# Low parts of the weights by an adding transfer, and a denser order of side work, in a one-core decoder trunk

## The chip, the cores and the metric

The kernel runs on one core of one Trainium2 chip. The metric is the device time of one execution in microseconds (us). The engines of a core are TensorE (PE, with its weight loads shown as PEld), VectorE (DVE), ScalarE (ACT), GpSimd (POOL) and SyncE (SP), which here issues most transfers (DMAs). Sixteen DMA engines serve all queues.

## The reference

One step of a hybrid decoder layer, for a prompt (16 meta tokens and 512 new ones) and 8 sample tokens that share the weights, 536 columns in all. Everything is float32.

```python
xn = rmsnorm(x, norm_gain)
h = einsum('btd,de->bte', xn, w_in)                 # 2048 -> 8704
q, k, v, z_a, u, z_s, g_a, g_s = split(h)
q, k = rope(rmsnorm(q)), rope(rmsnorm(k))
o_attn = sink_attention(q, k, v, window 128 + meta, sinks)   # 16 heads on 4 kv heads
y_ssm, state = s5_branch(u, ...)                    # diagonal complex scan, 64 groups x 64 states
y_ssm = gelu(y) * sigmoid(gelu(y) @ w_glu + b_glu)
br_a = (o_attn * silu(z_a)) @ w_attn_out
br_s = (y_ssm * silu(z_s)) @ w_ssm_out
y = x + (sigmoid(g_a) * br_a + sigmoid(g_s) * br_s) @ w_out
```

The outputs are y, the new keys and values, the final states, and the samples' updated windows.

## The kernel before

**Weights.** All weight matrices lie in one array `w` of units, each 128 x 8 x 128 values (512 KB). 176 units are streamed by `Stream`, and 32 more (w_out) by `Quads`, which forms 7 products for 8. TensorE multiplies float32r operands, so each weight is split into a high part `whi` (the cast) and a low part `wlo` (weight minus high part), and so are the activations (`xh`, `xl`). A product is three matmul passes: hi·hi, hi·lo and lo·hi. One unit is 48 matmuls of 260 or 268 columns on the line of `mm` (L901). `Stream.piece` makes a unit: SyncE loads `raw` (L783), ScalarE casts (L784), VectorE subtracts (L785). `Stream.get` makes units two ahead of the one that is handed out.

**Stages.** In the first 45 us the x tiles arrive, are scaled by the norm's gain and split, and three blocks are multiplied as they come (L988). Then follow blocks of two units each, in the order of the table `ORDER1`: `x` (a gate block, written to DRAM as gD), `u` (input of eight state-space blocks, each starting a generator `ssm`) and `h` (q, k and v rows, written to DRAM as rawD). Before, 42 blocks stand in that table. The remaining x blocks run beside attention. Then come w_glu (reads Y1), w_ssm_out (Y2), w_attn_out (A) and, through `Quads`, w_out (the line of `pr`, L1264).

**Side work.** `Background` holds generators in lanes. After each unit `mm` calls `bg.step(budget)`, which lets the generators issue work up to a number of units of VectorE time (BUDGET, and BUDGET2 to BUDGET4 in later stages). A generator yields the cost of what it has just issued, or None to end its turn. `ssm` is one such generator, `attention` another; `Attn.sample`, the sample tokens' attention, runs in the second lane. It reads the cached keys and values in pieces of 288 KB, and its loads are issued by GpSimd.

**Order.** The engines' queues are in order. The scheduler of the framework sets the order of each queue from the program order, a priority (the weights' work carries a high one) and its own estimate of time. SyncE's loads and stores, of weights and of side work, stand in one queue and reuse eight completion semaphores in turn, so a DMA waits until the eighth before it has landed.

**A state-space block.** u is evacuated to `uf`, split, written to DRAM (uD) and read back as `U` in another layout; `U` is read by the matmuls of L345 and L346; the scan runs on VectorE; L388, L392 and L396 form the block's output. GpSimd clears borders of U and H by memsets (L333, L340).

**Attention's start.** When the last state-space block is written, its memory is released and attention's tiles are loaded by SyncE: constants (k_cos and others), then for each of two pairs of kv heads the tiles sb, sw and rb of the keys, and the first query tiles. Two V tiles (L497) follow, which VectorE copies to `vb` (L501) and TensorE transposes (L505, L506). The first score matmul is L537.

Of the kernel before, what the change touches and what calls it, by code (L numbers as in the profile page):

```python
# [14 lines left out]
P = 128  # L15
# [208 lines left out]
def ssm_consts(nc, pool, psum, R, D, ub, a_bT, a_bN, a_cT, bdm):  # L224
# [26 lines left out]

    bN = pool.tile([P, 4, 2, 32], F32, name="bN")
    nc.sync.dma_start(out=bN, in_=a_bN[:, ps])
# [25 lines left out]
    v.tensor_tensor(out=k0, in0=bc(kp[:, 0, 0:32], 1, 4), in1=bc(bdm, 2, 32), op=ALU.mult)  # L279
    kh = pool.tile([P, P], F32R, name="kh")  # L280
    kl = pool.tile([P, P], F32R, name="kl")
    k0f = k0.rearrange("p a h -> p (a h)")
# [138 lines left out]
class Attn:  # L421
# [203 lines left out]
    def sample(self, a_sink, a_kc, a_vc):  # L625
# [3 lines left out]
        for c in range(2):  # L629
            cols = slice(4 * c, 4 * c + 4)  # L630
            src = self.raw[:, :, c, 264:268].rearrange("n p j -> p n j")
            nc.gpsimd.dma_start(out=x[:, :, cols], in_=src)
            for q in range(4):
                b = 32 * (q ^ 1)
                nc.gpsimd.dma_start(out=sw[32 * q:32 * q + 32, :, cols], in_=src[b:b + 32])
            for e in range(2):
                half = slice(64 * e, 64 * e + 64)
                for dst, r, w in ((rb[half, 4:12, cols], self.rq, 260), (rb[half, 0:2, cols], self.rk, CH)):
                    s = r[e::2, c * w + w - 4:c * w + w]
                    nc.gpsimd.dma_start(out=dst, in_=s.unsqueeze(0).to_broadcast([64] + list(s.shape)))  # L640
        co, si = C["cos"][:, 0, 264:265], C["sin"][:, 0, 264:265]
# [17 lines left out]
        for b in range(8):  # L659
            nc.gpsimd.dma_start(out=qD[:, b], in_=qt[8 * b:8 * b + 8])  # L660
        for i in range(2):
            for b in range(2):
                nc.gpsimd.dma_start(out=kD[i, :, b], in_=kt[16 * i + 8 * b:16 * i + 8 * b + 8])
        self.kD = kD
        q = pool.tile([P, 64], F32, name="qv", bufs=1)
        nc.gpsimd.dma_start(out=q, in_=qD.rearrange("s b (e d) -> (s b e) d", e=2))
        self.qv = q
        self.sk = pool.tile([P, 1], F32, name="sk", bufs=1)
        nc.gpsimd.dma_start(out=self.sk, in_=a_sink)
        yield 0.0  # L670
# [3 lines left out]
        def load(i, c, src):  # L674
            t = pool.tile([P, CK, 64], F32, name="cache")
            n = CK if c < 15 else CK - 1
            self.after = nc.gpsimd.dma_start(out=t[:, 0:n], in_=src[:, c * CK:c * CK + n]).ins
            if n < CK:
                new = self.kD[i].rearrange("s b (e d) -> (s b e) d", e=2)
                for r in range(4):  # L680
                    nc.gpsimd.dma_start(out=t[r::4, n], in_=new)
            return t
# [83 lines left out]
class Stream:  # L766


    def __init__(self, tc, nc, pool, w, ahead=2):
        self.tc, self.nc, self.pool, self.w, self.ahead = tc, nc, pool, w, ahead  # L770
        self.made, self.i, self.parts = 0, 0, {}

    def tiles(self, i, pool=None):
        raw = self.pool.tile([P, 8, P], F32, name="raw", bufs=3)
        hi = (pool or self.pool).tile([P, 8, P], F32R, name="whi", bufs=3)
        lo = (pool or self.pool).tile([P, 8, P], F32R, name="wlo", bufs=3)
        self.parts[i] = (hi, lo)
        return raw, hi, lo

    def piece(self, i, t, ks):  # L780
        nc = self.nc
        raw, hi, lo = (a[:, ks] for a in t)
        nc.sync.dma_start(out=raw, in_=self.w[i][:, ks])  # L783
        nc.scalar.copy(out=hi, in_=raw)  # L784
        self.dve = nc.vector.tensor_tensor(out=lo, in0=raw, in1=hi.bitcast(F32), op=ALU.subtract).ins  # L785
# [13 lines left out]
class Quads:  # L799
# [8 lines left out]

    def __init__(self, tc, nc, w, first, n, pool):
        self.tc, self.nc, self.w, self.first, self.n, self.pool = tc, nc, w, first, n, pool  # L810
        self.more = None
        self.loaded, self.made, self.i = 0, 0, 0
        self.raw, self.parts = {}, {}

    def load(self, upto):
        while self.loaded < min(upto, 4 * self.n):
            k = self.loaded
            pool, bufs = (self.pool, 3) if k % 7 < 3 else (self.more, 4)
# [36 lines left out]
def trunk(tc, A, O):  # L855
# [27 lines left out]
    nc.scalar.activation(out=warm, in_=warm, func=AF.Tanh)  # L883

    xn = tc.tile_pool(name="xn", bufs=1)
    xp = xn.__enter__()
# [3 lines left out]
    def mm(n, hi_of, lo_of, w0, budget=None, pool=mmp, name="mm"):  # L890
# [3 lines left out]
        for h in range(n):  # L894
# [47 lines left out]
    tmp = spp.__enter__()  # L942
    with tc.tile_pool(name="xld", bufs=2, side="right") as xld:
        ones = xld.tile([P, P], F32, name="ones", bufs=1)
        v.memset(ones, 1.0)
# [5 lines left out]
        def square(kt):  # L951
            sq = acc if kt == 0 else xld.tile([P, 2, CH], F32, name="xsq")
# [65 lines left out]
        for i, t in early:  # L1018
            evac(i, t)
        nx = NB0 + 2  # L1020
    C = {"idn": idn}
    bdm, dsk, bglu = const("bdm"), const("dsk"), const("bglu")
# [116 lines left out]
    def attended():  # L1139

        nonlocal late
        for i, (cache, out) in enumerate((("wk", "s_win_k"), ("wv", "s_win_v"))):
            with tc.issue_after(at.after):
                nc.gpsimd.dma_start(out=O[out][:, 0:127], in_=A[cache])
            nc.gpsimd.dma_start(out=O[out][:, 127], in_=at.kD[i].rearrange("s b d -> s (b d)"))
        att.__exit__(None, None, None)
# [74 lines left out]
    if late is None:  # L1221
        list(attended())
    xn.__exit__(None, None, None)
    Ah, Al = parts["a"]


    cbp = ent(tc.tile_pool(name="cbp", bufs=1))
    cb = []
    qs = Quads(tc, nc, A["w"], NUNIT, 8, wp)
    for i in range(16):  # L1230
# [208 lines left out]
```

## Time and profile before

| | |
|---|---|
| median of 3 runs | 1316.57 us (1316.45 to 1318.03) |
| profiled execution | 1317.95 us, of which the span of the profile is 1316.1 us |
| granted TensorE clock | 0.997 of full speed |
| busy | PE 1300.7 us, DVE 1003.5, ACT 443.5, POOL 52.4 |
| DMA | 209.70 MB, of which GpSimd's queue 13.89 MB |

A profile shows one execution. "Busy" is the time in which an engine executes; matmuls are pipelined, so a busy TensorE need not run at its best rate, and the number of matmuls that start in a window says more. In a timeline a row gives the start, the time to the end of the last of its instructions, the engine, the source line, the operation, output and inputs, a count, and in brackets the idle time ahead of it with what ended it. "SPq" is SyncE issuing a transfer, which lands later.

### The profile page before, as it was taken

The page shows a single profiled execution, that of the slowest core. Times are in us where ns is not written, and L with a number is a line of the kernel's source. Part 1 is how long each engine was busy: PE and PEld are TensorE (multiplying, and loading weights), DVE is VectorE, ACT ScalarE, POOL GpSimd, SP SyncE. Part 2 cuts the span into 40 slices and gives each one's busy share as a digit, 9 for nine tenths or more (in the row PEclk, how much of TensorE's full clock was granted, in tenths as well). Part 3 has the DMA queues.
Part 4 walks back from the last instruction along what each step waited for, and adds up shares of the span by engine and source line. Part 5 has one row for each costly group of instructions (what it writes and reads, how often), then busy time and mean ns, then how long its engine had stood idle before and what let it go on. Part 6 is the DMA issues. An engine that isn't in the chain of part 4 may idle for free.

```text
span 1316.1 us, 26574 instructions
## 1 busy us (share of the span) xinstructions
PE 1300.7 (99%) x10804; PEld 1259.9 (96%) x10804; DVE 1003.5 (76%) x1882; ACT 443.5 (34%) x742; POOL 52.4 (4%) x124
## 2 busy tenths in 40 slices
PE   9999999999999999999989999999999999999998
PEld 8999999999999999999989999999999999999998
DVE  7887788887969697968577688686885357888775
ACT  8322221223222222222254433334433133344342
POOL 0000000000000000000400210100011000000000
PEclk9999999999999999999989999999999999999999
DMA  8347363626353444343874346446677666554441
GB/s 268 123 136 212 104 186 115 187 92 184 110 166 116 155 122 153 97 152 125 190 228 131 107 153 193 131 133 205 194 226 247 203 194 189 159 199 142 151 145 50
DMA packets 95962, 209.70 MB, mean 159 GB/s; under 512 B 16556, under 2 KB 34972, under 8 KB 95808
## 3 DMA queue, kind: packets, MB, share of 16 engines
q1 hardware_dynamic: 91168, 194.11, 46.8%
q0 software_dynamic: 4672, 13.89, 4.0%
q8 instruction: 85, 1.39, 0.4%
q14 instruction: 37, 0.30, 0.1%
HBM read 175.32 MB, written 34.74 MB: 160 GB/s over the span
## 4 chain that ended last, share of the span: by engine, by line
PE 91%; DMA 3%; DVE 2%; ACT 1%; SPq 1%; issue 0%; POOL 0%; DVEq 0%; POOLq 0%; ACTq 0%
PE mm L901 70%; PE pr L1264 12%; PE aux L591 2%; PE mm L988 1%; DMA sw<-rawD 1%; PE aux L537 1%; PE aux L345 1%; PE aux L346 1%; PE aux L538 1%; PE aux L1065 1%; PE mm L1186 1%; PE aux L392 1%; PE aux L573 1%; DMA gD<-z 1%; DMA sb<-rawD 0%; ACT xh L979 0%
## 5 line engine op out<-in xcount | busy, mean ns | idle before, releaser
L901 PE MATMUL mm<-xh,whi 128*128 128x260 f32 (+1 forms) x2048 | 421.4, 286 | 0.0
L901 PE MATMUL mm<-xh,wlo 128*128 128x260 f32 (+1 forms) x2048 | 417.6, 285 | 0.0
L901 PE MATMUL mm<-xl,whi 128*128 128x260 f32 (+1 forms) x2048 | 416.3, 284 | 0.0
L784 ACT CAST whi<-raw 128x1024 fp32r<-128x1024 f32 (+3 forms) x188 | 186.1, 995 | 520.8 <-PE mm L901 346.7
L901 PEld LDWEIGHTS mm<-xh,whi 128*128 128x128 f32 x2048 | 318.2, 189 | 9.7 <-issue 9.3
L901 PEld LDWEIGHTS mm<-xl,whi 128*128 128x128 f32 x2048 | 318.5, 189 | 3.9 <-issue 3.9
L901 PEld LDWEIGHTS mm<-xh,wlo 128*128 128x128 f32 x2048 | 316.1, 188 | 4.2 <-issue 4.1
L785 DVE TENSOR_TENSOR wlo<-raw,whi 128x1024 fp32r<-128x1024 f32 (+3 forms) x188 | 215.5, 1151 | 43.8 <-ACT whi L784 41.8
L1264 PE MATMUL pr<-cb,whi 128*128 128x260 f32 x896 | 161.8, 283 | 1.3 <-DVE t L1244 1.3
L1264 PEld LDWEIGHTS pr<-cb,whi 128*128 128x128 f32 x896 | 138.1, 188 | 2.1 <-ACT whi L840 1.7
L901 PE MATMUL mm<-Y,whi 128*128 128x260 f32 x768 | 125.5, 284 | 0.0
L1264 PE MATMUL pr<-cb,wlo 128*128 128x260 f32 x448 | 125.5, 283 | 0.0
L901 PEld LDWEIGHTS mm<-Y,whi 128*128 128x128 f32 x768 | 105.7, 188 | 2.3 <-issue 2.3
L841 DVE TENSOR_TENSOR wlo<-raw,whi 128x1024 fp32r<-128x1024 f32 x56 | 67.1, 1223 | 23.0 <-ACT whi L840 21.3
L1264 PEld LDWEIGHTS pr<-cb,wlo 128*128 128x128 f32 x448 | 84.0, 188 | 0.0
L901 PE MATMUL mm<-A,whi 128*128 128x260 f32 x512 | 82.2, 282 | 0.0
L901 PE MATMUL mm<-Y,wlo 128*128 128x260 f32 x384 | 77.6, 283 | 0.0
L840 ACT CAST whi<-raw 128x1024 fp32r<-128x1024 f32 x56 | 57.7, 1049 | 55.1 <-DVE raw L839 21.0
L901 PEld LDWEIGHTS mm<-A,whi 128*128 128x128 f32 x512 | 70.2, 188 | 0.0
L928 DVE TENSOR_TENSOR z<-mm,R 128x520 f32<-128x520 f32 x43 | 30.0, 697 | 44.1 <-PE mm L901 42.5
L901 PEld LDWEIGHTS mm<-Y,wlo 128*128 128x128 f32 x384 | 59.2, 188 | 0.4 <-issue 0.4
L901 PE MATMUL mm<-A,wlo 128*128 128x260 f32 x256 | 51.6, 283 | 0.0
(377 smaller groups left out, 1496.6 us busy)
## 6 DMA issues: line engine op xcount, KB each, us to landing
raw<-in_w SPq DMA_DIRECT2D x202, 512.0 KB, 3.8
gD<-z SPq DMA_DIRECT2D x48, 260.0 KB, 2.2
t<-gD SPq DMA_DIRECT2D x32, 260.0 KB, 2.8
cache<-in_kc POOLq DMA_DIRECT2D x15, 288.0 KB, 3.5
cache<-in_vc POOLq DMA_DIRECT2D x15, 288.0 KB, 3.3
xr<-in_x SPq DMA_DIRECT2D x16, 268.0 KB, 5.5
sD<-z SPq DMA_DIRECT2D x16, 260.0 KB, 2.1
z<-sD SPq DMA_DIRECT2D x16, 260.0 KB, 3.0
```

What stands on the lines that cost most here:

```text
L345: nc.tensor.matmul(bu[:, i, 0:272], lhsT=D["bh"][:, i, a], rhs=U[:, a], start=True, stop=False)
L346: nc.tensor.matmul(bu[:, i, 0:272], lhsT=D["bl"][:, i, a], rhs=U[:, a], start=False, stop=True)
L392: nc.tensor.matmul(y[32 * a:32 * a + 32, 0, 0:NE], lhsT=D["cl"][:, a, i], rhs=H[:, a, i, 0:NE], start=False, stop=(i == 1), skip_group_che ...
L537: nc.tensor.matmul(ps[:, e, 0:272], lhsT=q, rhs=KH[:, k0:k0 + 272], start=True, stop=False)
L591: nc.tensor.matmul(pv[64 * e:64 * e + 64, 0, 0:256], lhsT=V[:, 64 * kv:64 * kv + 64], rhs=pr[:, e::2], start=(i == 0), stop=(i == len(part ...
L784: nc.scalar.copy(out=hi, in_=raw)
L785: self.dve = nc.vector.tensor_tensor(out=lo, in0=raw, in1=hi.bitcast(F32), op=ALU.subtract).ins
L840: nc.scalar.copy(out=hi, in_=t)
L841: nc.vector.tensor_tensor(out=lo, in0=t, in1=hi.bitcast(F32), op=ALU.subtract)
L901: m = nc.tensor.matmul(ps[:, c, 0:W], lhsT=wt[:, k], rhs=xo(kt, c), start=f, stop=l)
L928: v.tensor_tensor(out=z, in0=ps, in1=R_[:, :, 8:CH], op=ALU.mult)
L1264: nc.tensor.matmul(bank, lhsT=wt[:, p], rhs=cb[p][:, e, x], start=first and f and p == 0, stop=l and p == 7, skip_group_check=not first an ...
```

## The change

1. Units 10 to 162 (`BY_DMA`) are made another way. Each half of the unit is loaded into a small tile `half`; ScalarE writes the negated, rounded copy to `wlo` and the cast to `whi`; then GpSimd issues a DMA that reads the whole unit from DRAM again and adds it to `wlo`, which leaves weight minus high part. Every fourth unit takes its buffers from a further pool `wm`, and units are made three ahead.
2. `ORDER1` packs the eight u blocks and twelve h blocks into 34 blocks with fewer x blocks among them.
3. The budgets rise: 5.0, 4.8, 4.0 and 4.8 for 4.0, 3.6, 2.2 and 3.4. Side work is no longer held back behind VectorE's latest subtraction.
4. All loads and stores that GpSimd issued for the sample tokens, the updated windows and `zr` are issued by SyncE.
5. For memory, several tiles get fewer buffers (x tiles 8 for 10; bN, kh, kl, xsq one), and the raw tiles live in the start's pool and in a late pool `rwc`.

```diff
-BUDGET = 4.0
-BUDGET2, BUDGET3, BUDGET4 = 3.6, 2.2, 3.4
+BUDGET = 5.0
+BUDGET2, BUDGET3, BUDGET4 = 4.8, 4.0, 4.8
-NXR = 10
+NXR = 8
+BY_DMA = range(10, 163)
-for _u in range(8):
-    ORDER1 += [("u", _u), ("x", 0), ("x", 0)]
-    ORDER1 += [("h", 2 * _u), ("h", 2 * _u + 1)] if _u < 6 else [("x", 0), ("x", 0)]
+for _u in range(0, 8, 2):
+    ORDER1 += [("u", _u), ("x", 0)] + [("h", 3 * _u // 2 + i) for i in range(2)]
+    ORDER1 += [("u", _u + 1), ("x", 0), ("x", 0), ("h", 3 * _u // 2 + 2)]
...
-    def __init__(self, tc, nc, pool, w, ahead=2):
+    def __init__(self, tc, nc, pool, w, ahead=3):
...
     def make(self, i):
         with self.tc.high_priority(offset=HIGH):
-            self.piece(i, self.tiles(i), slice(0, 8))
+            if i not in BY_DMA:
+                self.piece(i, self.tiles(i), slice(0, 8))
+                return
+            nc = self.nc
+            _, hi, lo = self.tiles(i, self.more if i % 4 == 3 else None)
+            for ks in (slice(0, 4), slice(4, 8)):
+                raw = self.more.tile([P, 4, P], F32, name="half", bufs=2)
+                nc.sync.dma_start(out=raw, in_=self.w[i][:, ks])
+                nc.scalar.activation(out=lo[:, ks], in_=raw, func=AF.Copy, scale=-1.0)
+                nc.scalar.copy(out=hi[:, ks], in_=raw)
+            nc.gpsimd.dma_start(out=lo, in_=self.w[i], accum_op=ALU.add)
...
-            bg.after = (ws.dve,) if at is not None else ()
             bg.step(bud[0] if budget is None else budget)
...
-            nc.gpsimd.dma_start(out=x[:, :, cols], in_=src)
+            nc.sync.dma_start(out=x[:, :, cols], in_=src)
...
-            self.after = nc.gpsimd.dma_start(out=t[:, 0:n], in_=src[:, c * CK:c * CK + n]).ins
+            self.after = nc.sync.dma_start(out=t[:, 0:n], in_=src[:, c * CK:c * CK + n]).ins
...
-            nc.gpsimd.dma_start(out=zr, in_=gD[24 + b])
+            nc.sync.dma_start(out=zr, in_=gD[24 + b])
```

The order of SyncE's queue at attention's start, before: from the first query tiles (sw) to the second V load (the second row of L497). out_k is the new keys' output, gD a gate block, raw a weight unit.

```order
L446 DMA sw<-rawD 32x2x260
L474 DMA out_k<-sb 128x536
L446 DMA sw<-rawD 32x2x260 x3
L783 DMA raw<-in_w 128x1024
L446 DMA sw<-rawD 32x2x260 x4
L497 DMA sb<-rawD 128x536
L935 DMA gD<-z 128x520
L474 DMA out_k<-sb 128x536
L783 DMA raw<-in_w 128x1024
L497 DMA sb<-rawD 128x536
```

The same queue now, from the half load before the first V load to the second V load. x, s and r with a number are the sample's tiles (x12, s12, r12 in the code), half is half of a weight unit.

```order
L802 DMA half<-in_w 128x512
L497 DMA sb<-rawD 128x536
L952 DMA gD<-z 128x520
L802 DMA half<-in_w 128x512
L474 DMA out_k<-sb 128x536
L446 DMA sw<-rawD 32x2x260
L635 DMA s_8502<-rawD 32x12x4 x3
L640 DMA r_8503<-rqD 64x8x4
L640 DMA r_8503<-rkD 64x2x4
L802 DMA half<-in_w 128x512
L640 DMA r_8503<-rqD 64x8x4
L497 DMA sb<-rawD 128x536
```

The sample's loads and the half loads have come between the two V loads.

The head of SyncE's queue, before: x tiles, the gain and the first pieces of three weight units.

```order
L972 DMA xr<-in_x 128x536
L974 DMA gain<-in_gain 128x16
L783 DMA raw<-in_w 128x128 x3
L972 DMA xr<-in_x 128x536
L783 DMA raw<-in_w 128x128 x3
```

And now:

```order
L802 DMA half<-in_w 128x512 x2
L990 DMA xr<-in_x 128x536
L992 DMA gain<-in_gain 128x16
L789 DMA raw<-in_w 128x128 x3
L990 DMA xr<-in_x 128x536
L789 DMA raw<-in_w 128x128 x3
```

Both halves of unit 10 have moved ahead of the first x tile.

More of the change, by code (lines that the diff above doesn't have):

```diff
@@ L680, in load @@
                 for r in range(4):
-                    nc.gpsimd.dma_start(out=t[r::4, n], in_=new)
+                    nc.sync.dma_start(out=t[r::4, n], in_=new)
             return t
@@ L766, with tiles @@
 class Stream:
-    def __init__(self, tc, nc, pool, w, ahead=2):
+    def __init__(self, tc, nc, pool, w, ahead=3):
         self.tc, self.nc, self.pool, self.w, self.ahead = tc, nc, pool, w, ahead
         self.made, self.i, self.parts = 0, 0, {}
[L773 to L776, printed above, removed]
+        self.raw = self.more = None
+    def tiles(self, i, pool=None, raw=None):
+        pool = pool or self.pool
+        raw = self.raw.tile([P, 8, P], F32, name="raw", bufs=3) if self.raw else None
+        bufs = 1 if pool is self.more else 3
+        hi = pool.tile([P, 8, P], F32R, name="whi", bufs=bufs)
+        lo = pool.tile([P, 8, P], F32R, name="wlo", bufs=bufs)
         self.parts[i] = (hi, lo)
@@ L807, with __init__ @@
     SRC = (0, 1, 1, 1, 1, 3, 2)
-    def __init__(self, tc, nc, w, first, n, pool):
+    def __init__(self, tc, nc, w, first, n, pool, raws):
         self.tc, self.nc, self.w, self.first, self.n, self.pool = tc, nc, w, first, n, pool
-        self.more = None
+        self.more, self.raws = None, raws
         self.loaded, self.made, self.i = 0, 0, 0
@@ L1020, in trunk @@
         nx = NB0 + 2
+        ws.raw = None
     C = {"idn": idn}
@@ L1223, in trunk @@
     xn.__exit__(None, None, None)
+    wmc.__exit__(None, None, None)
+    rwc = ent(tc.tile_pool(name="rwc", bufs=1))
+    ws.more, ws.raw, ws.ahead = None, rwc, 2
     Ah, Al = parts["a"]
```

33 lines of the change are left out of this document (18 added, 15 removed).

## The prediction

> **What bounds the kernel now.** I read the first page for the engine that is never free, then windows of fifty microseconds for the stage in which it still loses time, then TensorE's timeline and SyncE's around that loss.
>
> The page gives the engines and the DMA queues; the windows give, for each stretch, busy time, granted clock, mean share of the 16 DMA engines, and GB/s:
>
> ```profile
> span 1316.1 us, 26574 instructions
> PE 1300.7 (99%) x10804; PEld 1259.9 (96%) x10804; DVE 1003.5 (76%) x1882; ACT 443.5 (34%) x742; POOL 52.4 (4%) x124
> q1 hardware_dynamic: 91168, 194.11, 46.8%
> ...
> core 0: us, PE busy (x) PEld busy (x) DVE busy (x) ACT busy (x) POOL busy (x), PEclk, DMA share, GB/s
> 0.00:50.00 50.00, 47.53 (x363) 46.30 (x364) 41.19 (x132) 32.55 (x58) 0.31 (x5) 1.00 0.69 223
> 425.00:490.00 65.00, 65.00 (x558) 62.34 (x557) 52.21 (x104) 17.29 (x23) 0.47 (x4) 1.00 0.45 138
> 626.00:657.00 31.00, 29.77 (x248) 29.56 (x246) 15.70 (x23) 8.41 (x14) 14.68 (x23) 1.00 0.83 196
> 650.00:700.00 50.00, 43.29 (x337) 42.05 (x336) 37.16 (x69) 23.35 (x59) 0.00 (x0) 0.93 0.65 194
> 1000.00:1050.00 50.00, 50.00 (x419) 50.00 (x418) 26.45 (x34) 13.75 (x17) 2.68 (x5) 1.00 0.68 223
> ```
>
> TensorE is busy for 99% of the span. Where nothing disturbs it, 419 matmuls start in 50 us, 0.12 us each, and the change leaves their number as it is (10485 matmul instructions in either program's order). VectorE, at 76%, is not what TensorE waits for on average, so a lighter VectorE is worth only the time that TensorE stands still. The one window with a real loss after the start is 650 to 700 us: 50 − 43.29 = 6.7 us idle, and a clock of 0.93, which is 3.5 us more; 10.2 us in all. TensorE's timeline shows it:
>
> ```profile
> 617.80 1.10 PE L396 MATMUL aux<-H,c 128*32 128x272 f32 x16
> ...
> 655.49 0.28 PE L901 MATMUL mm<-xh,wlo 128*128 128x260 f32 x1
> 661.04 1.12 PE L505 MATMUL aux<-k_idn,vb 128*128 128x128 f32 x4 [5.27 <-DVE vb L501]
> 661.95 0.42 PE L506 MATMUL aux<-k_idn,mt 128*64 128x128 f32 x1
> 662.39 0.64 PE L901 MATMUL mm<-xh,whi 128*128 128x260 f32 x2
> ...
> 676.16 0.39 PE L537 MATMUL aux<-KH,QT 128*128 128x272 f32 x1 [1.32 <-DVE QT L522]
> ```
>
> After the last state-space block (L396) comes the first transpose of attention's values (L505), 5.27 us late, and two matmuls afterwards take 0.64 us where two usually take 0.40. The first score (L537) is 1.32 us late. The next rows say why: SyncE's queue works through attention's loads in order, and the V tile's load is issued only at 657.10.
>
> ```profile
> 625.68 0.33 SPq L873 DMA_DIRECT2D k_cos<-in_cos  x1
> ...
> 657.10 0.52 SPq L497 DMA_DIRECT2D sb<-rawD  x1
> ...
> 661.12 0.32 SPq L497 DMA_DIRECT2D sb<-rawD  x1
> ...
> 657.10 3.37 DMA sb<-rawD
> 660.49 0.49 DVE vb L501 x2
> ```
>
> From the first constant of attention to the V load 38 DMAs are issued in 31.4 us: 0.827 us each. That pace, at a DMA share of 0.83, is the number on which my forecast rests.
>
> **The change part by part.** *The low parts.* Each of 153 units (10 to 162) loses one VectorE subtraction and one ScalarE cast and gets four ScalarE instructions on halves, a second SyncE load and a GpSimd DMA that adds.
>
> ```profile
> L785 DVE TENSOR_TENSOR wlo<-raw,whi 128x1024 fp32r<-128x1024 f32 x170 | 207.2, 1219 | 43.8 <-ACT whi L784 41.8
> L784 ACT CAST whi<-raw 128x1024 fp32r<-128x1024 f32 x170 | 178.6, 1050 | 520.7 <-PE mm L901 346.7 <-issue 155.5 <-DMA raw<-in_w 7.8
> L784 ACT CAST whi<-raw 128x512 fp32r<-128x512 f32 x9 | 5.0, 610 | 0.0
> L677 POOL DMA_DIRECT2D cache<-in_kc x16 | 8.7, 541 | 67.2 <-DVE ssc L686 57.3 <-DVE den L561 5.5 <-DVE m L551 1.8
> cache<-in_kc POOLq DMA_DIRECT2D x15, 288.0 KB, 3.5
> ```
>
> VectorE: 153 × 1.22 = 187 us less, to about 62% of the span. ScalarE: 153 × (4 × 0.61 − 1.05) = 213 us more, to about 50%. GpSimd: 153 × 0.54 = 83 us of issuing. None ends a wait of TensorE by its sum. What matters for TensorE is the chain of one unit: its buffers come free four units ahead of its use, so there are three units, 3 × 48 × 0.12 = 17.3 us; the chain is 4 × 0.61 + 0.54 us and a landing. No adding DMA stands in the trace. The nearest row is the GpSimd queue's load of 288 KB, 3.5 us; for 512 KB I take up to double, 7 us. That makes 10 us of the 17.3 and leaves 7, so I cost it at nothing: three units in stock hide it. If that cover goes, each microsecond late is a microsecond of TensorE per unit, up to 153 times.
>
> *What now stands behind a wait.* On GpSimd the adding DMAs stand behind the memsets of U and H, which wait for the block before; its row among the waits, and that of the sample's cache loads:
>
> ```profile
> POOL U L333 <- PE aux L346: 232.5, 6, 42.9
> POOL cache L677 <- DVE o_p L703: 65.5, 6, 29.0
> ```
>
> Those long waits cost nothing while GpSimd had nothing else. In the new order the matmul that each memset waits for stands within four matmuls of the one that frees the next unit's buffers, so the adding DMA loses 0.5 us of its 17.3. The cache loads now stand on SyncE with half loads behind them; a 29 us wait there would outlast the stock by 29 − 7 = 22 us. The order puts the weight work between them, so that they come later than GpSimd asked for them; I take 0.
>
> *The traffic.* Queue q1's 194.11 MB cost 46.8% of the span, 616 us of all 16 engines, so 512 KB (0.524 MB) cost 1.66 us. A state-space block now has 65 us and ten units, at a DMA share of 0.45: 29.3 us. After it has eight units in 65 × 8/10 = 52 us: 29.3 − 2 × 1.66 + 8 × 1.66 × f, where f is the price of an adding transfer against a plain one. f = 1 gives 39.3 us of 52 (76%), f = 2 gives 52.5 (101%), f = 3 gives 65.8 (127%). I have no row for f; a price below a plain load's has no reason, so 1 is the lower end, and I take between 1 and 2, near the plain load, as the nearest row.
>
> The Trainium skill's page Collectives: The Full Stack, in its section on the bandwidth ceiling, says that an adding transfer reads two sources for each chunk, and that the reads are what limits it. By that rule f is 2, each block would be 0.5 us over its time, and the second rival would be about to begin. No run here shows it yet.
>
> *The order of blocks.* Eight u blocks stand in 34 blocks instead of 42, with 5.0 instead of 4.0 units of side work after each weight unit. From the end of a u block to the first matmul that reads its U tile there are 144 matmuls of the mm line, where the last three blocks before had 192: up to 48 × 0.12 = 5.8 us less room. The room now is read from one block:
>
> ```profile
> 428.15 0.72 DVE L1098 TENSOR_TENSOR uf<-mm,R 128x536 f32<-128x536 f32 x1
> ...
> 438.25 0.42 SPq L336 DMA_DIRECT2D U<-uD  x1
> ...
> 451.50 0.29 PE L345 MATMUL aux<-U,bh 128*128 128x272 f32 x1
> ...
> U<-uD SPq DMA_DIRECT2D x16, 2.0 KB, 3.8
> ```
>
> U has landed at 438.25 + 3.8 = 442.05, 9.4 us early; 3.7 us remain. I cost this at nothing; two transfers in series, each slower by half, would use the 3.7 up. That attention ends sooner is worth nothing by itself: its result is written by 1017.3 us and first read at 1055.1.
>
> ```profile
> L1137 DVE TENSOR_TENSOR A<-oT,A x8: 689/698/701, 999.6 to 1017.3; 128x520 fp32r<-128x520 f32 x8
> L901 PE MATMUL mm<-A,whi x512: 277/282/287, 1055.1 to 1147.0; 128*128 128x260 f32 x171
> ```
>
> *Attention's start.* This is the largest term. The sample's small loads move from GpSimd's queue to SyncE's, and each weight unit has two loads there. Counted in the order of the program, 43 DMAs stand between k_cos and the first V load (38 before), 12 from that to the second V load (4 before), and the second row of Q norms is the tenth after it (third before). TensorE has more to do meanwhile: 332 matmuls between L396 and L505 (305 before), 34 between the two value groups (47), 81 from there to the first score (41). With the pace as it is:
> - first V: k_cos is issued 625.68 − 617.80 = 7.9 us after L396; + 43 × 0.827 = 35.6, + 3.4 landing, + 0.5 copy = 47.4 us. TensorE is there at 1.1 + 332 × 0.12 = 40.9. Wait 6.5 us.
> - second V: 12 × 0.827 = 9.9 us later, against 1.0 + 34 × 0.12 = 5.1 of work. Wait 4.8 us.
> - first score: before, 676.16 − 661.12 = 15.0 us passed from the second V load to it, of which 5.7 to the issue of the norms' second load (666.8) and 9.3 after; now 10 × 0.827 + 9.3 = 17.6, against 3.9 + 1.0 + 81 × 0.12 = 14.6. Wait 3.0 us.
>
> The row behind that 666.8 (the second of two):
>
> ```profile
> 666.22 1.20 SPq L449 DMA_DIRECT2D rb<-rqD  x2
> ```
>
> Together 14.3 us idle instead of 6.7. The slow clock after it was 3.5 us for one long wait; with two waits of that length it is between 3.5 and 7, and I take 5.2. So 19.5 against 10.2: +9.3 us. Bounds by the pace: SyncE's bare issue takes about 0.5 us (0.52 above), which leaves only 0.9 us of wait, −9.3 us net. Upward, the adding transfers bring 31/6 = 5.2 units × 1.66 to 3.3 us into the window of 31 us whose share is already 0.83, up to 1.39; a pace of 1.15 us gives waits of 20.4 + 8.7 + 6.2 us and a clock loss of 7, +32 us.
>
> The Trainium skill's page TensorE: Matmul & The Clock Gate (Part 1, the HAM clock gate) says that an idle window of about 3.4 us puts the array back to half clock. The 0.64 us after the 5.27 us wait agrees. By it both long waits would pay, and the term would be +11.1.
>
> *The start.* The program now opens SyncE's queue with two half loads of unit 10, before the first x tile. That is two issues, 2 × 0.42 = 0.84 us, up to the 0.524 MB at the 223 GB/s of the first window, 2.35 us; between them, +1.6 us, since TensorE waits for these loads there:
>
> ```profile
> 1.66 1.38 SPq L783 DMA_DIRECT2D raw<-in_w  x3
> ```
>
> Eight x buffers instead of ten delay only the last x tiles, which TensorE reaches last and with a backlog (47.53 us busy of the first 50): 0, at most the 2.35 us again. The other memory edits (one buffer for bN, kh, kl, the raw pools moved) touch tiles whose readers are a whole block away: 0.
>
> The sum: +9.3 + 1.6 = +10.9 us on the profiled execution's 1317.95 us, 1328.9. The median of the runs is 1316.57, 1.4 lower; so 1327.5.
>
> **The rivals.** *Faster: the V tiles arrive in time.* GpSimd's 18 small loads no longer run beside the K rows (in 626 to 657 GpSimd is busy for 14.68 us), VectorE is freer, and SyncE goes at its issue pace. It decides at a pace of 0.66 us or less, where the waits come to about 5 us. At 0.5 us: 1316.57 − 9.3 + 0.84, about 1308. Against it: the share of 0.83 in that window, with traffic added.
>
> *DMA saturates.* If f is between 2 and 3, state-space blocks stretch to the transfers' time. It decides at f = 2. At 2.5 it is 59.1 − 52 = 7 us in each of eight blocks, 56 us, which makes 1383 with the forecast's terms. For it: nothing in the trace bounds f from above. Against it: three units of stock, and a window at 0.83 in which no weight was waited for.
>
> *Nothing measurable.* A pace of 0.7 us: waits 1.0 + 3.3 + 1.7, half of the clock loss, 7.8 against 10.2, and + 1.6: 1315.7.
>
> **How the numbers follow.** Forecast (slower, 1327.5; 1320 to 1351): 0.47. Faster, about 1308: 0.31. Saturated, 1350 and up: 0.12. Nothing: 0.10. A measurement of this kernel tells about 0.2% (2.6 us) from no change. Slower: 0.47 + 0.12 = 0.59. The range goes from 1307.2 (all 10.2 us won back, the start at 0.84) to 1351 (pace 1.15, the start at 2.35); it leaves out the saturated case and the ends of the others.
>
> **What would show it.** Right: in the new profile L505 waits for vb twice, 6.5 and 4.8 us, and SyncE needs 0.8 us or more for each DMA between k_cos and the V load; no wait of the mm line for wlo. Wrong: L505 without a wait (the faster rival), or mm matmuls waiting for the adding DMA with a DMA share near 1 in the state-space blocks (the saturated one).

## The result, and the profile after

The changed kernel takes 1520.06 us (median; 1505.62 to 1529.35 over 4 runs), the one before 1316.51 us: 1.1507 times as long, with a 95% interval of 1.1427 to 1.1588. The longest of the four ran in a slower state of the chip and is left out of the ratio. The change is slower, as forecast, but by 204 us instead of 11, and far outside the range.

The profiled execution took 1505.62 us. The first page of the changed kernel, engines and DMA queues (packets, MB, share of the 16 engines' span):

```profile
span 1503.8 us, 27572 instructions
PE 1355.4 (90%) x10804; PEld 1304.9 (87%) x10804; DVE 835.5 (56%) x1729; ACT 622.1 (41%) x1201; POOL 137.3 (9%) x193
...
q1 hardware_dynamic: 128896, 208.01, 44.2%
q0 software_dynamic: 22032, 80.23, 30.9%
```

TensorE, busy for 1300.7 of 1316.1 us before, is now idle for 1503.8 − 1355.4 = 148.4 us, 133 more. And it is busy for 54.7 us more with the same 10804 matmuls, since its mean clock was 0.951: the trace's record of the granted clock has 28 stretches at half speed, 147 us of the span (before: 2, 9 us). Together that is 187.7 us, the whole difference of the spans. Windows by stage, changed kernel:

```profile
core 0: us, PE busy (x) PEld busy (x) DVE busy (x) ACT busy (x) POOL busy (x), PEclk, DMA share, GB/s
0.00:50.00 50.00, 46.50 (x358) 46.11 (x358) 39.25 (x113) 32.96 (x59) 0.31 (x5) 0.97 0.64 213
150.00:500.00 350.00, 324.75 (x2724) 311.56 (x2723) 233.96 (x521) 139.88 (x250) 43.43 (x71) 0.97 0.84 203
600.00:1000.00 400.00, 338.43 (x2518) 313.44 (x2516) 206.51 (x433) 175.43 (x459) 38.88 (x47) 0.92 0.77 189
1050.00:1250.00 200.00, 176.76 (x1390) 173.52 (x1390) 35.27 (x52) 79.47 (x140) 24.16 (x28) 0.95 0.89 227
1250.00:1500.00 250.00, 245.65 (x2024) 244.63 (x2023) 187.83 (x212) 93.99 (x116) 0.00 (x0) 0.99 0.50 160
```

And one of them before:

```profile
150.00:500.00 350.00, 350.00 (x2993) 335.51 (x2992) 289.41 (x566) 94.99 (x119) 2.56 (x22) 1.00 0.46 143
```

The loss lies in every stage that has adding transfers: 25 us idle in 350 of the state-space blocks, 62 in 400 of attention, 23 in 200 of w_glu and w_ssm_out. Behind 1250 us, where none is left, TensorE runs almost as before. The DMA engines' mean share in the state-space stage went from 0.46 to 0.84. It is not 1.

What TensorE waited for, from the page of waits (total us, times, longest):

```profile
PE aux L573 <- DVE Pm L565: 19.8, 6, 5.3
PE aux L505 <- DVE vb L501: 14.1, 2, 10.2
PE aux L276 <- DVE bb L269: 11.1, 1, 11.1
...
PE mm L919 <- DMA wlo<-in_w: 9.3, 9, 2.2
...
PE aux L345 <- DMA bN<-in_bN: 6.8, 2, 3.6
```

The adding DMA itself is named for 9.3 us. Most of the rest are matmuls of the side work (`aux`): they wait for operands whose loads or whose ScalarE steps came late. What ScalarE and SyncE's queue waited for:

```profile
SPq L802 <- ACT wlo L803: 327.4, 116, 23.0
SPq L802 <- DMA half<-in_w: 171.4, 88, 10.4
...
ACT whi L804 <- DMA half<-in_w: 445.0, 163, 11.5
...
ACT wlo L803 <- DMA half<-in_w: 52.5, 20, 6.1
```

ScalarE stood still for 497 us until a half load had landed, with side work behind that cast in its queue; before, it waited 7.8 us for weight loads. One block's timeline shows what this does to the U tile (uf is the block's u as VectorE leaves it, uh its cast, U the load that the first L345 needs; the bracket of L345 names whi, a cast that it doesn't read, while the last of its U loads was issued 5.0 us before it):

```profile
355.66 0.72 DVE L1117 TENSOR_TENSOR uf<-mm,R 128x536 f32<-128x536 f32 x1 [2.02 <-PE mm L919]
...
359.80 1.21 ACT L804 CAST whi<-half 128x512 fp32r<-128x512 f32 x2 [3.42 <-DMA half<-in_w]
...
362.91 0.63 ACT L324 CAST uh<-uf 128x536 fp32r<-128x536 f32 x1
...
374.98 0.41 SPq L334 DMA_DIRECT2D U<-uD  x1
375.48 0.39 SPq L802 DMA_DIRECT2D half<-in_w  x1
375.93 0.48 SPq L335 DMA_DIRECT2D U<-uD  x1
377.52 0.32 SPq L336 DMA_DIRECT2D U<-uD  x1
...
382.52 0.57 PE L345 MATMUL aux<-U,bh 128*128 128x272 f32 x1 [6.64 <-ACT whi L804]
```

From uf to the last U load 377.52 − 355.66 = 21.9 us pass. In the block that the prediction showed, it was 438.25 − 428.15 = 10.1. There the cast uh followed uf within 0.8 us:

```profile
428.90 0.64 ACT L324 CAST uh<-uf 128x536 fp32r<-128x536 f32 x1
```

Now it comes 7.3 us later, behind casts that wait for a half load; the rest passes in SyncE's queue, between uh and the last load of U. Read in the same way in all eight blocks, that stretch is 17.3 us in the mean now and 11.8 before; of it, uf to uh is 4.4 us now and 2.0 before. The prediction had left 3.7 us of room there.

### The profile page after: what moved, and what is told of

Read it like the earlier page. It is cut to its first block, busy times and chain, and to the rows that moved or that the text cites. A ratio compares the mean times of both kernels' runs of the same rounds, so it can differ in the third digit from the quotient of the medians.

```text
span 1503.8 us, 27572 instructions
## 1 busy us (share of the span) xinstructions
PE 1355.4 (90%) x10804; PEld 1304.9 (87%) x10804; DVE 835.5 (56%) x1729; ACT 622.1 (41%) x1201; POOL 137.3 (9%) x193
## 4 chain that ended last, share of the span: by engine, by line
DMA 30%; PE 27%; issue 7%; ACT 6%; DVE 5%; SPq 2%; POOL 1%; ACTq 0%; POOLq 0%; DVEq 0%
DMA half<-in_w 18%; PE mm L919 15%; PE pr L1286 10%; ACT wlo L803 3%; DMA cache<-in_vc 3%; DMA cache<-in_kc 2%; ACT whi L804 1%; DMA wlo<-in_w 1%; DMA f<-FD 1%; DMA uD<-uh 1%; DMA sb<-rawD 1%; DVE o_p L703 1%; PE aux L591 1%; POOL wlo L805 1%; DMA zr<-gD 1%
## 5 line engine op out<-in xcount | busy, mean ns | idle before, releaser
L919 PE MATMUL mm<-xh,whi 128*128 128x260 f32 (+1 forms) x2048 | 436.1, 294 | 0.3 <-ACT xr L979 0.3
L919 PE MATMUL mm<-xh,wlo 128*128 128x260 f32 (+1 forms) x2048 | 427.1, 290 | 6.5 <-ACT KH L488 4.0
L919 PE MATMUL mm<-xl,whi 128*128 128x260 f32 (+1 forms) x2048 | 428.5, 290 | 0.0
L804 ACT CAST whi<-half 128x512 fp32r<-128x512 f32 x306 | 185.1, 617 | 508.6 <-DMA half<-in_w 445.0
L919 PEld LDWEIGHTS mm<-xh,whi 128*128 128x128 f32 x2048 | 331.1, 196 | 10.8 <-issue 8.6
L919 PEld LDWEIGHTS mm<-xh,wlo 128*128 128x128 f32 x2048 | 327.2, 195 | 10.9 <-issue 6.7
L919 PEld LDWEIGHTS mm<-xl,whi 128*128 128x128 f32 x2048 | 331.2, 196 | 5.7 <-issue 5.6
L805 POOL DMA_DIRECT2D wlo<-in_w x153 | 132.2, 864 | 1052.1 <-ACT wlo L803 864.9
L803 ACT ACTIVATE wlo<-half 128x512 fp32r<-128x512 f32 x306 | 177.3, 622 | 52.6 <-DMA half<-in_w 52.5
L919 PEld LDWEIGHTS mm<-Y,whi 128*128 128x128 f32 x768 | 110.1, 196 | 20.2 <-DVE z L1223 11.0
```

What stands on the lines that cost most here:

```text
L803: nc.scalar.activation(out=lo[:, ks], in_=raw, func=AF.Copy, scale=-1.0)
L804: nc.scalar.copy(out=hi[:, ks], in_=raw)
L805: nc.gpsimd.dma_start(out=lo, in_=self.w[i], accum_op=ALU.add)
L919: m = nc.tensor.matmul(ps[:, c, 0:W], lhsT=wt[:, k], rhs=xo(kt, c), start=f, stop=l)
```

## The experiments

All ratios are to the kernel before, run beside each on the same chip. Three theories stand against each other: the added transfers delay all other loads (traffic); half loads that wait for one of two buffers hold up the queues (queue, later called ring, after the ring of half buffers); the new order leaves the side work too little room (order). Where a kernel issues other instructions, the scheduler also reorders others; e4 and after, and e14 and e9, have the same order on every engine and in SyncE's queue.

**e1, low parts by VectorE, all else as after.** The raw tiles take the memory of the halves.

```diff
-BY_DMA = range(10, 163)
+BY_DMA = range(0)
...
-    def __init__(self, tc, nc, pool, w, ahead=3):
+    def __init__(self, tc, nc, pool, w, ahead=2):
...
+            bg.after = (ws.dve,) if at is not None else ()
...
-        ws.raw = xld
+        ws.raw = ws.more
```

> All low parts by VectorE again, whole raw loads with three buffers, side work held back behind the subtraction as before; the new order of blocks, the new budgets and the loads moved to SyncE stay. Traffic theory (the adding DMA's transfers fill the DMA engines and delay every other load): 1310 to 1335 us, DMA share about 0.5 in the state-space blocks. Queue theory (half loads that wait for one of two buffers hold up SyncE's queue): the same, 1310 to 1335. Order theory (blocks of 52 us with 5.0 units of side work leave side matmuls too little room, whatever makes the low parts): 1440 or more, TensorE still waiting for U, bb and V.

Measured: 1317.26 us, ratio 1.0001 (0.9991 to 1.0010). Taken together, the order of blocks, the larger budgets and the loads moved to SyncE cost and gain nothing. (`Quads` also prepares two units ahead in it, for three; its stage, behind 1150 us, shows no loss.)

**e2, the other way round:** the adding DMA alone, with before's ORDER1, budgets and GpSimd loads.

```diff
-BUDGET = 5.0
-BUDGET2, BUDGET3, BUDGET4 = 4.8, 4.0, 4.8
+BUDGET = 4.0
+BUDGET2, BUDGET3, BUDGET4 = 3.6, 2.2, 3.4
...
-            self.after = nc.sync.dma_start(out=t[:, 0:n], in_=src[:, c * CK:c * CK + n]).ins
+            self.after = nc.gpsimd.dma_start(out=t[:, 0:n], in_=src[:, c * CK:c * CK + n]).ins
...
```

> The other way round: low parts by the adding DMA as after, but the order of blocks and the budgets of before, and the sample's loads on GpSimd as before. Traffic theory: 1400 to 1480, since the added traffic is the same 153 units, with a somewhat lower share in blocks of 65 us. Queue theory: 1420 to 1500. Order theory: 1320 to 1350.

Measured: 1492.01 us, 1.1323 (1.1306 to 1.1340). So 174 us of the 198 come with the low parts alone, and the order theory falls; the remaining 24 us appear only where the low parts and the new order meet.

**e3, one eighth of the adding traffic.**

```diff
-            nc.gpsimd.dma_start(out=lo, in_=self.w[i], accum_op=ALU.add)
+            nc.gpsimd.dma_start(out=lo[:, 0:1], in_=self.w[i][:, 0:1], accum_op=ALU.add)
```

> As after, but the adding DMA covers one eighth of each unit (seven eighths of the low part keep the negated weight): 153 x 64 KB instead of 153 x 512 KB of adding traffic, with the half loads, the casts, the queues and the blocks as they are. Traffic theory: 1320 to 1360, DMA share in the state-space stage down from 0.83 to about 0.55. Queue theory and order theory: 1460 or more.

Measured: 1343.17 us, 1.0192 (1.0175 to 1.0209), as the traffic theory had it.

**e4, a plain second transfer:**

```diff
-            nc.gpsimd.dma_start(out=lo, in_=self.w[i], accum_op=ALU.add)
+            nc.gpsimd.dma_start(out=lo, in_=self.w[i])
```

> As after in every queue, but the second transfer does not add: it writes the weight over the low part. Same bytes, same instructions, same order. In after's trace an adding packet of 4096 bytes took 327 ns at the median, a plain one 159. Traffic theory: more than half of the loss goes, 1360 to 1430, share in the state-space stage about 0.70. Queue and order theories: 1460 or more, since only the price of a packet changes.

Measured: 1428.04 us, 1.0843 (1.0795 to 1.0892). Its packets of 4096 bytes took 174 ns at the median, after's adding ones 327. So the size and then the price of the second transfer decide most of it: 25 us with an eighth of it, 111 with a plain one, 198 with an adding one (ratios less 1, times 1316.6). I took the traffic theory for shown here, and e5 and e6 corrected me.

**e5, four half buffers instead of two**, and three weight buffers, on the kernel of e3 (units are made two ahead, and unit 162 goes to VectorE):

```diff
-                raw = self.more.tile([P, 4, P], F32, name="half", bufs=2)
+                raw = self.more.tile([P, 4, P], F32, name="half", bufs=4)
...
-            _, hi, lo = self.tiles(i, self.more if i % 4 == 3 else None)
+            _, hi, lo = self.tiles(i)
```

> The kernel with one eighth of the adding traffic (1343 us; seven eighths of each low part keep the negated weight), now with four half buffers instead of two and three weight buffers instead of four. In its trace ScalarE stood still for 223 us until a half load landed, with side work behind the cast in its queue; before, it hardly ever waited for a weight load. If that is where its remaining 26 us come from: 1318 to 1332, that wait below 80 us, and the waits of attention's matmuls and of the weights at 930 to 1000 us gone. If they come from the 213 us of casts that ScalarE has to do in addition: 1338 or more. Two more half loads ahead of the first x tile may cost up to 2.4 us at the start in either case.

Measured: 1334.84 us, 1.0157 (1.0127 to 1.0188), between the two cases. ScalarE's wait until a half lands is no longer among its longest (240 us before the casts are put down to nothing that the profile shows); the start costs more (TensorE busy for 44.59 us of the first 50 at a clock of 0.93; in e3 46.95 at full clock). Part of e3's loss, then, is the ring of buffers.

**e6, traffic that nobody waits for**, on the kernel of e1:

```diff
+        if 10 <= i < 163:
+            junk = self.junk.tile([P, 8, P], F32, name="junk", bufs=2)
+            nc.gpsimd.dma_start(out=junk, in_=lo.bitcast(F32))
```

> Low parts by VectorE (the kernel of 1317 us), and beside it GpSimd writes each finished low part of units 10 to 162 to DRAM, 512 KB each, read by nobody: transfers alone, on which no matmul waits. If the transfers' share of the DMA engines is the cause, this gets near the kernel with a plain second transfer (1428): 1375 to 1440, TensorE late at the side work (U, bN, V, cache). If the loss comes from the chain (half loads, casts, the landing that each low part waits for): below 1335.

Measured: 1332.36 us, 1.0119 (1.0105 to 1.0133). That is the second case: 512 KB more per unit, with a share of 0.71 from 150 to 500 us, the same as in e4, cost 16 us where e4 lost 111. The share alone does not explain e4's loss. The transfers are not quite alike, though: these go from SBUF to DRAM, those of e4 from DRAM to SBUF.

**e7, every second unit by the adding DMA**, the others from two raw buffers, with units made two ahead:

```diff
-BY_DMA = range(10, 163)
+BY_DMA = range(11, 163, 2)
...
```

> Every second unit by the adding DMA (76 units), the others by VectorE with two raw buffers. A loss in proportion to the traffic: about 1317 + 203 / 2 = 1418. A loss that grows with the share of the DMA engines (about 0.65 in a state-space block instead of 0.83): 1330 to 1375.

Measured: 1377.94 us, 1.0469 (1.0449 to 1.0489), by 3 us above the range for a steep growth. TensorE was busy for only 41.50 of the first 50 us (e1: 47.66), because raw loads came ahead of the x tiles. Without these 6 us, half of the traffic costs 56 us, well under half of 198.

**e8, attention's start put off**, on the kernel of e1:

```diff
...
+        yield None
+        yield None
+        with self.later():
+            for b in range(4):
+                nc.tensor.transpose(out=ps[:, 0, 128 * b:128 * b + 128], in_=vb[:, b], identity=self.C["idn"])
...
         at.load_q(0)
         yield None
+        yield None
+        yield None
```

> Low parts by VectorE and the new order (1317 us), and attention's start put off: each of the two value steps ends two turns after its load and has its transposes behind the latest weight matmul, and two more turns stand ahead of the first scores. In the trace of the kernel without this, TensorE waited 3.5 us for vb and 1.1 for the first scores and then had 3.4 us at half clock. If these go and nothing takes their place: 1317 - 3.5 - 1.1 - 1.7 to 3.4 = 1309 to 1311. If the wait only moves to the next step of attention: 1315 or more.

Measured: 1313.76 us, 0.9978 (0.9969 to 0.9987): faster than both kernels by 0.2%, about half of what was hoped. One wait of 3.0 us for vb is left.

**e9, whole raw loads, three buffers, and the adding DMA.** The ring of the kernel before under the low parts of after:

```diff
-            _, hi, lo = self.tiles(i, self.more if i % 4 == 3 else None)
-            for ks in (slice(0, 4), slice(4, 8)):
-                raw = self.more.tile([P, 4, P], F32, name="half", bufs=2)
...
+            raw, hi, lo = self.tiles(i)
+            nc.sync.dma_start(out=raw, in_=self.w[i])
+            nc.scalar.activation(out=lo, in_=raw, func=AF.Copy, scale=-1.0)
+            nc.scalar.copy(out=hi, in_=raw)
```

It also has half as many loads and casts as after, and three weight buffers, so that units are made two ahead.

> The adding DMA as after, for all 153 units, but the weights come as before: one load of 512 KB into one of three raw buffers, two whole casts, three weight buffers. Ring theory (two half buffers hold one unit in all, so each load's longer landing under traffic stops SyncE's and ScalarE's queues, and the side work behind the halves comes late): most of the 203 us goes, 1340 to 1400, and ScalarE's 445 us until a half load lands falls below 150. Traffic theory (the adding transfers delay all loads, whatever the buffers): 1460 or more.

Measured: 1419.66 us, 1.0773 (1.0733 to 1.0813): between the two, half of the loss gone. Of ScalarE's waits for a load none is among the seven longest; 262 us before its casts are put down to nothing that the profile shows (before: 156), so that the 150 us of the expectation can't be read off cleanly. With the smaller stock TensorE now waits 20.6 us for the adding DMA itself, where after waits 9.3.

**e10, two plain writes per unit that nobody waits for** (e6's write twice):

```diff
+            junk = self.junk.tile([P, 8, P], F32, name="junk", bufs=4)
+            nc.gpsimd.dma_start(out=junk, in_=lo.bitcast(F32))
```

> Low parts by VectorE, and GpSimd writes each finished low part to DRAM twice: 2 x 512 KB of plain packets (159 ns each) for units 10 to 162, which is the DMA time of one adding transfer (327 ns a packet), with no matmul waiting for them. One such write cost 15 us. If the share of the DMA engines alone decides (it should come to 0.85 or more, as after): 1440 or more. If the share costs much only together with the ring of two half buffers: 1335 to 1390.

Measured: 1362.71 us, 1.0353 (1.0322 to 1.0384), as the ring theory had it.

**e11, more turns ahead of attention's start** than in e8:

```diff
-        yield None
-        yield None
+        for _ in range(4 - e):
+            yield None
```

> As the kernel of 1313.8 us, with four turns instead of two between the first value step's load and its transposes, and three at the second. There the only large wait left was 3.0 us for vb at 562 us, and 1.7 us of slow clock behind it. If it goes and nothing follows it: 1308.5 to 1310.5. If the scheduler moves the load along with its matmuls: 1313 or more.

Measured: 1312.87 us, 0.9979 (0.9970 to 0.9987), no better than e8. The wait for vb is gone and the clock full there, but 1.0 and 1.9 us of waits stand at 910 and 921 us in its place.

**e12, after with four half buffers** and three weight buffers, by e5's edit of the halves, with the adding DMA on the whole unit (and unit 162 by VectorE):

> As after, with four half buffers instead of two, paid for with the fourth weight buffer (units are made two ahead instead of three). Ring theory: part of the loss goes, 1400 to 1470, although the adding DMA has a unit less of stock. Traffic theory: 1500 or more, since the traffic is the same and the stock smaller.

Measured: 1444.08 us, 1.0948 (1.0915 to 1.0980): two more half buffers win back 74 us although the stock of finished units is smaller. In its profiled execution (1457.42 us) ScalarE's wait until a half lands, ahead of whi, is 33.1 us, for 445.0; 196 us there are put down to nothing that the profile shows.

**e13 and e14, the whole loads of e9 with one eighth of the adding traffic (e3's edit), and with a plain second transfer (e4's edit):**

```diff
 e13
+            nc.gpsimd.dma_start(out=lo[:, 0:1], in_=self.w[i][:, 0:1], accum_op=ALU.add)
 e14
+            nc.gpsimd.dma_start(out=lo, in_=self.w[i])
```

> Whole loads into three raw buffers, two whole casts per unit, and the adding DMA on one eighth of the unit (seven eighths of the low part keep the negated weight): the casts and the landing without the traffic. If the casts are a large part of the 57 us: 1340 to 1375. If they lie beside other work, as the prediction had it: 1317 to 1328. With two half buffers the same traffic gave 1343.

> The kernel with whole loads (1420 us), with a second transfer that writes the weight over the low part instead of adding it; the order of all instructions is the same. If the landing and the traffic's share decide: about 1317 + 15 (plain traffic that nobody waits for) + what the casts cost by the run beside this one, 1335 to 1355. If waiting for the landing is costly in itself, plain or adding: 1380 or more.

Measured: e13 1326.54 us, 1.0064 (1.0049 to 1.0080); e14 1350.69 us, 1.0268 (1.0241 to 1.0295). Both as the cheap case had it: casts and landing cost little.

**e15, the adding transfer that nobody waits for**, on the kernel of e1:

```diff
+        if 10 <= i < 163:
+            acc = dict(accum_op=ALU.add) if i > 11 else {}
+            nc.gpsimd.dma_start(out=self.junk[i % 2], in_=lo.bitcast(F32), **acc)
```

> Low parts by VectorE, and GpSimd adds each finished low part of units 10 to 162 to one of two arrays in DRAM, 512 KB each, read by nobody: the adding transfer without casts and without anyone who waits. Two plain writes of the same share cost 46 us. If an adding transfer is no more than its time in the DMA engines: 1345 to 1375. If it delays the other loads by more than that: 1390 or more.

Measured: 1392.30 us, 1.0584 (1.0559 to 1.0609): dearer than two plain writes at the same share. Windows from 150 to 500 us, of e1, e10, e15 and e9 in this order:

```profile
150.00:500.00 350.00, 350.00 (x3047) 336.20 (x3046) 319.98 (x638) 97.53 (x123) 3.03 (x26) 1.00 0.46 146
```

```profile
150.00:500.00 350.00, 338.63 (x2903) 323.56 (x2902) 310.14 (x616) 92.93 (x118) 56.79 (x128) 0.99 0.86 292
```

```profile
150.00:500.00 350.00, 323.29 (x2698) 309.17 (x2697) 288.35 (x578) 84.45 (x107) 42.85 (x71) 0.96 0.86 203
```

```profile
150.00:500.00 350.00, 329.72 (x2789) 315.87 (x2789) 242.62 (x537) 134.60 (x161) 44.84 (x73) 0.97 0.84 209
```

At 0.84 to 0.86 of the DMA engines' time TensorE loses 11 us of these 350 with plain writes (e10), 27 (e15) and 20 (e9) with adding transfers. GpSimd's queue, in which memsets stand behind the adding DMAs, could have a part in e15's loss. The memsets of U have none: in e15 those that each block's first L345 needs were done before that block's uf. That of H and the longer hold on the `wlo` buffers (7.8 us to landing, 6.6 in e10) were not separated.

**e16, the kernel before with e8's edit at attention's start:**

```diff
+        yield None
+        yield None
+        with self.later():
...
```

> The kernel before, untouched but for attention's start: two more turns ahead of each value step's transposes, which stand behind the latest weight matmul, and two more ahead of the first scores. Its trace has 10.2 us of waits and slow clock there. If that loss goes and attention, which ended 38 us before it was needed, is still in time: 1306 to 1310. If the added turns (6 x 5.8 us) make attention the late one: 1314 or more.

Measured: 1314.93 us, 0.9987 (0.9978 to 0.9996). That lies in the range of the second case, but attention is not late: a wait of 3.8 us for vb is left. Some of e8's gain is there without the new order of blocks; what the order adds is too small to tell, since the intervals overlap.

Ratios put together, less 1 and times 1316.6 us:

| second transfer | one eighth, adding | plain | adding |
|---|---|---|---|
| two half buffers | +25 (e3) | +111 (e4) | +198 (after) |
| three raw buffers | +8 (e13) | +35 (e14) | +102 (e9) |
| low part by VectorE, nobody waits | 0 (e1, none) | +16 (e6) | +77 (e15) |

Read by the last column, the loss of 198 us is 77 for the adding transfers as mere traffic, 25 more for the casts and the landing, and 96 more for the ring of two half buffers. These are differences between kernels and not three separate prices: e15's transfers go from SBUF to DRAM, e9 has less stock, and after has twice e9's loads and casts. e12 keeps the halves and their casts and still wins 74 of the 96, so most of that part is the depth of the ring. The ring costs little without traffic (25 − 8 = 17 us), 76 with a plain transfer, 96 with an adding one: it is the pair that is dear. Two half buffers hold one unit; as landings get longer, the next half load waits for a cast, the cast for a landing, and SyncE's and ScalarE's queues stand still with the side work behind them. The traces agree in part: from uf to uh pass 4.4 us in the mean in after, 1.5 in e9 and 0.9 in e15.

By stage, after is longer than e9 by 35 us from 50 us to the last state-space block (549 for 514), by 33 in attention from the first L505 to the first matmul that reads Y (421 for 388), and by 15 from there to the first that reads A (162 for 147). The U tile shown above is a sign of the ring, but not where most of it is paid: TensorE's waits on the line of L345 are 28.9 us in after and still 24.9 in e9. Which tiles carry the 96 us was not traced further.

## Why the prediction was wrong, step by step

**The low parts, "I cost it at nothing: three units in stock hide it": the step that failed.** The landing it assumed was about right:

```profile
L805 POOL DMA_DIRECT2D wlo<-in_w x153 | 132.2, 864 | 1052.1 <-ACT wlo L803 864.9 <-DVE h0b L214 58.2 <-PE mm L919 35.3
...
wlo<-in_w POOLq DMA_DIRECT2D x153, 512.0 KB, 7.6
```

7.6 us, for 7 estimated; 0.86 us of GpSimd per issue, for 0.54. The stock held too, in the stage for which it was worked out: for units 20 to 84 the adding DMA was issued 16.6 us ahead of the unit's first matmul (median). Only for the last, units 150 to 162, was that 8.0 us, hardly more than the landing. But the chain that I costed begins when the weight buffers are free, and the half loads ahead of it have a ring of one unit, not three. I never asked which queues stand still while that ring waits. By the runs: 96 us for the ring (74 of them by e12 alone), 25 for casts and landing.

**The traffic, "f between 1 and 2, near the plain load", and "it decides at f = 2".** The price was mis-sized: 327 ns against 159 for a packet of 4096 bytes, f = 2.06; in the prediction's own unit, all packets of 512 KB, it is 0.309 × 1503.8 / 153 = 3.04 us against 1.66, f = 1.83. The sentence from the Trainium skill's page Collectives: The Full Stack (the bandwidth ceiling), that an adding transfer reads two sources and that reads limit it (the page says it of a collective's reduction), agrees with these rows better than my choice did. The heavier mistake was the threshold. By 1.83 a block's transfers take 50.3 of its 52 us, so the sum still said nothing lost. I let the DMA engines be free of cost up to a share of 1; e10 and e15 lose 46 and 77 us at 0.86, with no matmul waiting for the added transfers.

**The order of blocks, "3.7 us remain; I cost this at nothing; two transfers in series, each slower by half, would use the 3.7 up".** The condition was named and then came true: from uf to the last U load, 17.3 us instead of 11.8. Without the traffic (e1) it is 10.6 us, its page of waits has 0.2 us for L345, and the term is nothing, as costed.

**Attention's start, +9.3 us.** The forecast's waits were 6.5, 4.8 and 3.0 us. SyncE's queue and TensorE, changed kernel:

```profile
597.91 1.10 PE L396 MATMUL aux<-H,c 128*32 128x272 f32 x16
...
612.17 0.33 SPq L889 DMA_DIRECT2D k_cos<-in_cos  x1
...
648.17 0.42 SPq L497 DMA_DIRECT2D sb<-rawD  x1
...
655.68 1.11 PE L505 MATMUL aux<-k_idn,vb 128*128 128x128 f32 x4 [10.16 <-DVE vb L501]
...
666.51 0.66 PE L505 MATMUL aux<-k_idn,vb 128*128 128x128 f32 x4 [3.93 <-DVE vb L501]
...
682.74 0.59 PE L537 MATMUL aux<-KH,QT 128*128 128x272 f32 x1 [4.19 <-DVE QT L522]
```

Here they are 10.2, 3.9 and 4.2. The pace was right, 36.00 us for 43 DMAs, 0.837 each; k_cos was issued 14.3 us after L396 instead of 7.9. But that is a pace under the added traffic. In e1, the new order without it:

```profile
535.49 0.33 SPq L889 DMA_DIRECT2D k_cos<-in_cos  x1
...
560.88 0.40 SPq L497 DMA_DIRECT2D sb<-rawD  x1
```

```profile
PE aux L505 <- DVE vb L501: 3.3, 1, 3.3
...
PE aux L537 <- DVE QT L522: 1.0, 1, 1.0
```

40 DMAs in 25.4 us, 0.635 each, and 4.3 us of waits: the faster rival's condition (0.66 or less) and nearly its waits (about 5 us, though the sum's own terms give 4.1 at that pace; 6.6 before). So the pace behind the largest term of my sum held here only under the low parts' loads and transfers, which I had costed at nothing; the new order of the queue alone does not give it.

**The clock.** I gave it 5.2 us for two waits. TensorE stalled 28 times for more than 2 us, the record has 28 slow stretches, and slower matmuls cost 54.7 us, more than a quarter of the loss. The Trainium skill's page TensorE: Matmul & The Clock Gate (Part 1, the HAM clock gate) has an idle window of about 3.4 us; the trace's slow stretches are 3.4, 6.8 or 10.2 us long (one, at the span's end, is cut short by it), which agrees.

**The start, +1.6 us.** TensorE was busy for 46.50 us of the first 50 instead of 47.53, and the clock fell to 0.97 there: 1.0 us idle and up to 1.5 of clock, near the term.

**What held.** An earlier end of attention was worth nothing: in e1 its result is written by 865.5 us instead of 1018.0, at a ratio of 1.0001. A lighter VectorE showed no gain either: e13 has no subtraction for the 153 units and little added traffic, and takes 1.0064, though its added casts may hide one. Of the rivals, the saturated one (0.12) had the direction and the right suspect; its mechanism, transfers beyond the time of a block, did not occur, and its 1383 us is 137 too low.

## What to carry to other kernels

A mean share of the DMA engines is not a budget to be filled up to 1: at 0.86 the loads of chains with a few us of room were late, block after block. When an operation gets one more step, follow the ring that feeds it back to its first load, count that ring's depth in units of work, and list what stands in each in-order queue behind its waits. And where TensorE is busy for 99%, look for the one place that isn't: putting attention's first matmuls two turns later brought 0.1 to 0.2% (e16, e8, e11), where a kernel with 153 subtractions less on VectorE was no faster (e13).

## What the runs showed of the hardware

An adding packet of 4096 bytes from DRAM to SBUF took 327 ns at the median (after), a plain one on the same queue 174 (e4), and one from SBUF to DRAM 159 (e6). At an equal share of 0.86, adding transfers cost more than plain ones (77 us in e15 against 46 in e10), for a reason that these runs leave open. GpSimd spent 0.86 us on issuing a 512 KB adding DMA, and 0.53 on a plain one (e4). And in the changed kernel 133 us of added idle time, most of it in stalls of 2 to 11 us, came with 54.7 us of slower matmuls, about 40% again.
